# First x tiles and first weight columns loaded ahead of the recurrence constants in a two-stage hybrid block

## The chip, the cores and the metric

One core of a Trainium2 chip runs the whole kernel. The metric is the device time of one execution in microseconds. Engines are named as in the profile: PE (TensorE, with PEld for its weight loads), DVE (VectorE), ACT (ScalarE), POOL (GpSimd), and SP (SyncE, which issues nearly all DMAs).

## The reference

The input is x, 2048 tokens of width 1024, in float32; 16 learned meta tokens are put ahead of it and dropped at the end. One layer is computed:

```
h += rms_norm(W_out [RG-LRU | forgetting attention | RWKV-7](W_in rms_norm(h)))
h += rms_norm(W_down(gelu(g) * v)),   [g | v] = causal_dwconv3(W_up rms_norm(h))
```

W_in has 3080 columns: 512 feed the RG-LRU group ("a"), 3 x 512 are queries, keys and values ("q", "k", "v") with 8 forget-gate columns, and 1024 feed the RWKV-7 group ("c"). The RG-LRU and RWKV-7 groups are recurrences over the tokens.

## The kernel before, in words

Matrix products in float32 precision are made of three matmuls (`mm3`): each operand is split into a high part (rounded to fp32r by ACT) and a low part (the rest, by DVE).

The input projection works in three parts of the tokens, each with two blocks of up to 400 tokens (part 0: the meta rows and tiles x1 to x3, then tiles x4 to x6). `w_in_norm` calls `norm_transpose` for every tile of 128 tokens: a load into a slot of the pool "nt" (four slots, shared with raw weight columns), the sum of squares on ACT (L118), the reciprocal root by three Newton steps on DVE (`rstd_from`, L85 to L94; with `core.apart` the steps run on POOL, L90 and L91), the scaling by the root and the gain `g_pre` on DVE (L130), eight 128x128 transposes on PE (L143), and the evacuation into a high part (ACT, L149) and a low part (DVE, L150).

`w_in_part` is a generator that then runs over the columns: first the forget gate (`w_in_gate`, L287 and L288), then units of 128 columns. For a unit, `w_in_weights` loads the columns (L165), splits them (L166 on ACT, L167 on DVE) and, in part 0, keeps both halves in DRAM for the later parts (L216). `w_in_step` multiplies them with each block (24 matmuls, L172 to L174) and stores the result in a scratch in DRAM (L243 for "a" and "c"). The last two units run block by block together.

The driver builds the first `READY = 13` steps of that generator, then the constants of the recurrences (`attn_consts`, `rwkv_consts`, `lru_consts`, `columns`: short vectors loaded by SP, L848, transposed on PE, L854, copied on DVE, L855; weights at L895 to L898 and L1355; the series of `lru_consts` on DVE, L1368 and L1369), and then goes on with the generator while the recurrences (L993 to L1440; their first matmul is L1034) are woven in beside it. They take their intermediate tiles from the pool "rp", where the tag "rw_sc" has two slots. Attention, output projection and the feed-forward stage follow.

The order in which each engine issues is not the order of this code alone: a scheduler with a timeline of its own arranges the instructions, under their dependencies and in the order written where it sees no reason against it. Each engine then works its list in order. `tc.issue_after(ins)` puts what is written inside it behind `ins` on that instruction's engine.

The lines that order the start are these:

```
following = w_in_norm(core, pools, ps_mm, x, meta, g_pre, 0)
...
units = w_in_part(core, pools, ps_mm, a["w_in"], blocks, scr, part)
for _ in range(READY if part == 0 else 0):
    next(units)
if part == 0:
    attn_consts(core)
    rk = rwkv_consts(...)
```

Of the kernel before, what the change touches and what calls it, by code (L numbers as in the profile page):

```python
# [8 lines left out]
F32 = mybir.dt.float32  # L9
# [3 lines left out]
AF = mybir.ActivationFunctionType  # L13
# [108 lines left out]
def norm_transpose(core, pools, psum, src, rows, gain, pieces):  # L122

    nc = core.nc
    xt = pools["nt"].tile([P, D], F32, tag="nt_x", name=core.n("xt"))
    nc.sync.dma_start(xt[:rows], src)
    junk = pools["st"].tile([P, D], BF16, tag="stv", name=core.n("xj"), bufs=1)
    v = pools["nt"].tile([P, 6], F32, tag="rs", name=core.n("rs"))
    rs = rstd_of(core, v[:rows], xt[:rows], D, junk[:rows])
    nc.vector.scalar_tensor_tensor(xt[:rows], xt[:rows], rs, gain[:rows], op0=ALU.mult, op1=ALU.mult)  # L130
    transpose_split(core, psum, xt, rows, pieces)
# [21 lines left out]
def split_load(core, pool, raws, src, shape, tag):  # L153

    hi = pool.tile(shape, F32R, tag=tag + "h", name=core.n(tag + "h"))
    lo = pool.tile(shape, F32R, tag=tag + "l", name=core.n(tag + "l"))
    load_parts(core, raws, src, hi[:], lo[:])
    return hi, lo


def load_parts(core, raws, src, hi, lo):

    pool, tag, bufs = raws
    raw = pool.tile(list(hi.shape), F32, tag=tag, name=core.n("raw"), bufs=bufs)
    core.loaded = core.nc.sync.dma_start(raw[:], src)  # L165
    core.nc.scalar.activation(hi, raw[:], AF.Copy)  # L166
    core.nc.vector.tensor_tensor(lo, raw[:], hi, op=ALU.subtract)  # L167


def mm3(nc, out, ah, al, bh, bl, first, last, more=False):  # L170
# [3 lines left out]
    nc.tensor.matmul(out, al, bh, start=False, stop=last, skip_group_check=more)  # L174
# [12 lines left out]
def w_in_norm(core, pools, psum, x, meta, gain, part):  # L187
    blocks = []
    for b, tl in enumerate(w_in_tokens(part)):
# [4 lines left out]
        blocks.append((t0, n, tl, hi, lo))  # L194
    for t0, n, tl, hi, lo in blocks:
        for s, rows in tl:
            src = meta if s < META else x[s - META : s - META + rows, :]
            norm_transpose(core, pools, psum, src, rows, gain, [(hi, lo, s - t0, 0, rows)])
    return blocks

# [6 lines left out]
def w_in_weights(core, pools, w_in, c0, scr, part):  # L207

    if part == 0:
        src = w_in[:, c0 : c0 + P].rearrange("(k p) c -> p k c", p=P)  # L210
        pair = split_load(core, pools["w"], (pools["nt"], "nt_x", None), src, [P, KD, P], "w")
# [8 lines left out]
def w_in_step(core, pools, psum, weights, block, kind, c0, scr):  # L220
# [6 lines left out]
    for k in range(KD):  # L227
        mm3(nc, ps[:, :n], wh[:, k], wl[:, k], hi[:, k], lo[:, k], k == 0, k == KD - 1)
# [68 lines left out]
def w_in_part(core, pools, psum, w_in, blocks, scr, part):  # L297
    yield from w_in_gate(core, pools, psum, w_in, blocks, scr, part)
# [11 lines left out]
    for kind, c0 in units[:-2]:  # L310
# [4 lines left out]

    last = [(w_in_weights(core, pools, w_in, c0, scr, part), kind, c0) for kind, c0 in units[-2:]]
    for block in blocks:
        for w, kind, c0 in last:
            step(w, block, kind, c0)
        yield  # L320
# [1592 lines left out]

WIDE = (0, 5)
# [61 lines left out]
def hybrid_block_kernel(ctx: ExitStack, tc: tile.TileContext, args, out):  # L1976
# [25 lines left out]
    with ExitStack() as p1:  # L2002
# [7 lines left out]
        with ExitStack() as p1a:  # L2010
            ps_mm = pool(p1a, "ps_mm", 5, space=PSUM)
            g_pre = spread(pool(p1a, "gpre", 1), a["norm_mix_pre"], "g_pre")
# [3 lines left out]
            following = w_in_norm(core, pools, ps_mm, x, meta, g_pre, 0)  # L2016
            for part in range(3):
# [6 lines left out]
                units = w_in_part(core, pools, ps_mm, a["w_in"], blocks, scr, part)  # L2024
                for _ in range(READY if part == 0 else 0):
                    next(units)
                if part == 0:
                    attn_consts(core)
                    rk = rwkv_consts(
# [14 lines left out]
                    columns(core, gp, ps_ae, [a["ffn_conv"].rearrange("i (r p) -> (i r) p", p=P)], "", cw)  # L2044
                    R = Rwkv(core, rp, dp, ps_rw, ps_ae, scr, rk)
# [168 lines left out]
```

## Time and profile before

| what | value |
|---|---|
| runs | 3072.16 us median of 3 (3068.99 to 4877.26) |
| profiled execution, span from first to last instruction | 3071.8 us |
| PE busy | 2921.6 us, 95% |
| PE weight loads busy | 2495.2 us, 81% |
| DVE busy | 2054.8 us, 67% |
| ACT busy | 1482.3 us, 48% |
| POOL busy | 1358.8 us, 44% |
| DMA, mean over the span | 173 GB/s |

How to read it: the span is the profiled execution's own time, and no other time of that execution is given. A busy share is a mean over stages with different limits; a stage's own limit is read from a window of it. In a row of a group or of the timeline, "out<-in" are the tiles written and read, and the bracket names what ended the idle time before the instruction. SPq is SP's queue of DMA issues. Lines such as L130 are lines of the kernel before.

### The profile page before, as it was taken

What the parts mean: (1) busy time and instruction counts of PE and PEld (TensorE: products, weight loads), DVE (VectorE), ACT (ScalarE), POOL (GpSimd) and SP (SyncE); (2) the same over time, 40 slices, a digit from 0 to 9 for tenths busy, and PEclk for the clock granted to TensorE, in tenths of its full rate; (3) what the DMA queues carried; (4) which work ended last, traced back from release to release, by engine and by line L of the source; (5) the groups of instructions that cost most, each with busy time, mean ns of one, the idle gap of its engine ahead of it and who ended that gap; (6) DMA issues with size and microseconds to landing.
All of it is one profiled execution on the core that took longest, in us unless ns stands there. A gap on an engine that the chain in (4) does not pass through costs nothing. (4 is left out here: it accounts for less than half of the span.)

```text
span 3071.8 us, 52793 instructions
## 1 busy us (share of the span) xinstructions
PE 2921.6 (95%) x18694; PEld 2495.2 (81%) x18694; DVE 2054.8 (67%) x3934; ACT 1482.3 (48%) x2853; POOL 1358.8 (44%) x1589
## 2 busy tenths in 40 slices
PE   6999999999989999999989899999999999999998
PEld 6998898888876654665558899999999998787876
DVE  5268645656667785556635788888778786547766
ACT  4245332443336553555534656666566665324333
POOL 1001121122114555667842457445655444547765
PEclk9998999999988898999999999999999999999999
DMA  6776578466654346535245555566777765435444
GB/s 211 244 237 207 161 244 287 156 211 204 196 153 94 88 104 199 133 99 122 62 129 173 168 182 180 169 201 208 214 215 216 219 189 171 161 104 171 149 160 144
DMA packets 467818, 532.58 MB, mean 173 GB/s; under 512 B 85488, under 2 KB 355514, under 8 KB 466000
## 3 DMA queue, kind: packets, MB, share of 16 engines
q1 hardware_dynamic: 467168, 528.81, 56.5%
q8 instruction: 147, 2.41, 0.3%
q14 instruction: 119, 0.97, 0.1%
q0 software_dynamic: 384, 0.39, 0.0%
HBM read 369.11 MB, written 159.95 MB: 172 GB/s over the span
## 5 line engine op out<-in xcount | busy, mean ns | idle before, releaser
L172 PE MATMUL psu<-xo,uw 128*128 128x344 f32 x1848 | 589.9, 323 | 16.7 <-ACT xo L1594 6.9
L173 PE MATMUL psu<-xo,uw 128*128 128x344 f32 x1848 | 592.6, 321 | 0.0
L174 PE MATMUL psu<-xo,uw 128*128 128x344 f32 x1848 | 582.9, 320 | 0.0
L172 PE MATMUL psp<-xh,wh 128*128 128x384 f32 (+2 forms) x1152 | 383.6, 333 | 4.1 <-ACT wh L166 2.4
L174 PE MATMUL psp<-xh,wl 128*128 128x384 f32 (+2 forms) x1152 | 380.7, 331 | 3.5 <-DMA wl<-scr_wk 3.5
L173 PE MATMUL psp<-xl,wh 128*128 128x384 f32 (+2 forms) x1152 | 380.5, 330 | 0.0
L172 PEld LDWEIGHTS psu<-xo,uw 128*128 128x128 f32 x1848 | 346.9, 188 | 20.3 <-ACT xo L1594 7.1
L1595 DVE TENSOR_TENSOR uw<-uq,uw 128x512 fp32r<-128x512 f32 x341 | 316.2, 933 | 70.3 <-ACT uw L1594 63.7
L173 PEld LDWEIGHTS psu<-xo,uw 128*128 128x128 f32 x1848 | 347.9, 188 | 0.3 <-DVE xo L1595 0.3
L174 PEld LDWEIGHTS psu<-xo,uw 128*128 128x128 f32 x1848 | 346.5, 188 | 0.0
L1594 ACT ACTIVATE uw<-uq 128x512 fp32r<-128x512 f32 x462 | 287.9, 627 | 110.1 <-PE psu L174 48.7
L686 ACT ACTIVATE p<-sc,bias 128x512 f32<-128x512 f32 (+4 forms) x352 | 195.8, 590 | 178.5 <-PE sc L682 146.3
L1725 DVE SCALAR_TENSOR_TENSOR uy<-psu,ffn_cols,uy 128x342 f32<-128x342 f32 (+1 forms) x396 | 223.9, 567 | 60.7 <-ACT uy L1723 59.1
L559 DVE TENSOR_REDUCE mc<-mx 128x1 f32<-128x512 f32 (+6 forms) x352 | 190.3, 565 | 100.9 <-PE mx L554 75.8
L1731 POOL TENSOR_TENSOR uy<-uy,uy 128x342 f32<-128x342 f32 (+1 forms) x132 | 140.6, 1065 | 253.2 <-DVE uy L1725 77.4
L725 POOL TENSOR_TENSOR acc<-acc,p 128x512 f32<-128x512 f32 (+3 forms) x208 | 221.8, 1068 | 60.3 <-ACT p L686 23.9
L1595 POOL TENSOR_TENSOR uw<-uq,uw 128x512 fp32r<-128x512 f32 x121 | 177.9, 1470 | 125.0 <-ACT uw L1594 92.7
L174 PEld LDWEIGHTS psp<-xh,wl 128*128 128x128 f32 x1152 | 222.1, 193 | 13.0 <-issue 6.1
L172 PEld LDWEIGHTS psp<-xh,wh 128*128 128x128 f32 x1152 | 222.1, 193 | 10.7 <-issue 4.0
L173 PEld LDWEIGHTS psp<-xl,wh 128*128 128x128 f32 x1152 | 222.1, 193 | 7.6 <-issue 5.5
L1595 DVE TENSOR_TENSOR fo<-u,fo 128x896 fp32r<-128x896 f32 x88 | 112.6, 1279 | 121.3 <-ACT fo L1594 121.3
L1594 ACT ACTIVATE fo<-u 128x896 fp32r<-128x896 f32 x88 | 81.1, 922 | 206.3 <-POOL u L1841 106.8
(465 smaller groups left out, 6470.4 us busy)
## 6 DMA issues: line engine op xcount, KB each, us to landing
uq<-scr_us SPq DMA_DIRECT2D x220, 256.0 KB
uq<-in_ffn_up_dram SPq DMA_DIRECT2D x209, 256.0 KB
wl<-scr_wk SPq DMA_DIRECT2D x48, 512.0 KB
wh<-scr_wk SPq DMA_DIRECT2D x48, 512.0 KB
u<-scr_ff SPq DMA_DIRECT2D x88, 256.0 KB
scr_ff<-uy SPq DMA_DIRECT2D x110, 171.0 KB
raw<-in_w_in_dram SPq DMA_DIRECT2D x24, 512.0 KB
scr_wk<-wh SPq DMA_DIRECT2D x24, 512.0 KB
```

The lines of the kernel that those rows point to most:

```text
L172: nc.tensor.matmul(out, ah, bh, start=first, stop=False, skip_group_check=more)
L173: nc.tensor.matmul(out, ah, bl, start=False, stop=False, skip_group_check=more)
L174: nc.tensor.matmul(out, al, bh, start=False, stop=last, skip_group_check=more)
L559: self.reduced = nc.vector.tensor_reduce(mc[:rows, i, ci : ci + 1], ps[:rows, : e - a], axis=AX.X, op=ALU.max)
L686: last = nc.scalar.activation(p[:rows, :w], ps[:rows, :w], AF.Exp, bias=bias[:rows, j : j + 1])
L725: eng.tensor_tensor(a, ps_[0][0][:rows, c0:n] if start and i == 1 else a, p[:rows, : n - c0], op=ALU.add)
L1594: core.nc.scalar.activation(hi, src, AF.Copy)
L1595: (eng or core.nc.vector).tensor_tensor(lo, src, hi, op=ALU.subtract)
L1725: stt(y[:, :n], src[:, i : n + i], cw[:, 44 * i + cc : 44 * i + cc + 1], y[:, :n], op0=ALU.mult, op1=ALU.add)
L1731: core.pooled = nc.gpsimd.tensor_tensor(v[:, :n], g[:, :n], v[:, :n], op=ALU.mult)
```

## The change

A new function `first_loads` issues the first loads in an order of its own: x1, x2, the gain, x3, the meta rows, the first weight columns, x4 to x6, the second weight columns. The six x tiles go into two tiles of the recurrences' tag "rw_sc" (three x tiles each) in place of slots of "nt". `w_in_norm` takes them from there, treats the meta rows as the last tile of the first block, and sets `core.apart`, so that the Newton steps of part 0 run on POOL. `w_in_part` runs the first two units ("c") ahead of the forget gate in part 0, block by block together. The constants of the recurrences are put behind the last weight transfer, the last matmul and the last weight split that were built when the generator had made its fifth step.

```diff
@@ -119,11 +119,12 @@
     return rstd_from(core.nc, v, ss, width, core.apart)
 
 
-def norm_transpose(core, pools, psum, src, rows, gain, pieces):
+def norm_transpose(core, pools, psum, src, rows, gain, pieces, xt=None):
 
     nc = core.nc
-    xt = pools["nt"].tile([P, D], F32, tag="nt_x", name=core.n("xt"))
-    nc.sync.dma_start(xt[:rows], src)
+    if xt is None:
+        xt = pools["nt"].tile([P, D], F32, tag="nt_x", name=core.n("xt"))
+        nc.sync.dma_start(xt[:rows], src)
     junk = pools["st"].tile([P, D], BF16, tag="stv", name=core.n("xj"), bufs=1)
     v = pools["nt"].tile([P, 6], F32, tag="rs", name=core.n("rs"))
     rs = rstd_of(core, v[:rows], xt[:rows], D, junk[:rows])
@@ -150,20 +151,21 @@
             nc.vector.tensor_tensor(lo[:, ks, ds_], ps[:, :, ss_], hi[:, ks, ds_], op=ALU.subtract)
 
 
-def split_load(core, pool, raws, src, shape, tag):
+def split_load(core, pool, raws, src, shape, tag, raw=None):
 
     hi = pool.tile(shape, F32R, tag=tag + "h", name=core.n(tag + "h"))
     lo = pool.tile(shape, F32R, tag=tag + "l", name=core.n(tag + "l"))
-    load_parts(core, raws, src, hi[:], lo[:])
+    load_parts(core, raws, src, hi[:], lo[:], raw)
     return hi, lo
 
 
-def load_parts(core, raws, src, hi, lo):
+def load_parts(core, raws, src, hi, lo, raw=None):
 
     pool, tag, bufs = raws
-    raw = pool.tile(list(hi.shape), F32, tag=tag, name=core.n("raw"), bufs=bufs)
-    core.loaded = core.nc.sync.dma_start(raw[:], src)
-    core.nc.scalar.activation(hi, raw[:], AF.Copy)
+    if raw is None:
+        raw = pool.tile(list(hi.shape), F32, tag=tag, name=core.n("raw"), bufs=bufs)
+        core.loaded = core.nc.sync.dma_start(raw[:], src)
+    core.parted = core.nc.scalar.activation(hi, raw[:], AF.Copy)
     core.nc.vector.tensor_tensor(lo, raw[:], hi, op=ALU.subtract)
 
 
@@ -171,7 +173,7 @@
 
     nc.tensor.matmul(out, ah, bh, start=first, stop=False, skip_group_check=more)
     nc.tensor.matmul(out, ah, bl, start=False, stop=False, skip_group_check=more)
-    nc.tensor.matmul(out, al, bh, start=False, stop=last, skip_group_check=more)
+    return nc.tensor.matmul(out, al, bh, start=False, stop=last, skip_group_check=more)
 
 
 
@@ -184,7 +186,7 @@
     return [tiles[a:e] for a, e in zip(cuts, cuts[1:])]
 
 
-def w_in_norm(core, pools, psum, x, meta, gain, part):
+def w_in_norm(core, pools, psum, x, meta, gain, part, landed={}):
     blocks = []
     for b, tl in enumerate(w_in_tokens(part)):
         t0 = tl[0][0]
@@ -192,23 +194,60 @@
         hi = pools["xn"].tile([P, KD, n], F32R, tag=f"xh{b}", name=core.n("xh"))
         lo = pools["xn"].tile([P, KD, n], F32R, tag=f"xl{b}", name=core.n("xl"))
         blocks.append((t0, n, tl, hi, lo))
+    core.apart = bool(landed)
     for t0, n, tl, hi, lo in blocks:
-        for s, rows in tl:
+        for s, rows in tl[1:] + tl[:1] if t0 == 0 else tl:
             src = meta if s < META else x[s - META : s - META + rows, :]
-            norm_transpose(core, pools, psum, src, rows, gain, [(hi, lo, s - t0, 0, rows)])
+            norm_transpose(core, pools, psum, src, rows, gain, [(hi, lo, s - t0, 0, rows)], landed.get(s))
+    core.apart = False
     return blocks
 
 
+def first_loads(core, pools, gpool, rpool, x, meta, gain, w_in):
+
+    nc = core.nc
+    landed = {}
+    tiles = [t for tl in w_in_tokens(0) for t in tl]
+    g = gpool.tile([P, D], F32, name="g_pre")
+
+    def rows_of(some):
+        if len(some) > 1:
+            three = rpool.tile([P, 3, D], F32, tag="rw_sc", name=core.n("x0"), bufs=2)
+        else:
+            three = pools["nt"].tile([P, 1, D], F32, tag="nt_x", name=core.n("xt"))
+        for i, (s, rows) in enumerate(some):
+            nc.sync.dma_start(three[:rows, i], meta if s < META else x[s - META : s - META + rows, :])
+            landed[s] = three[:, i]
+            yield
+
+    early, late, ahead = rows_of(tiles[1:4]), rows_of(tiles[4:7]), []
+    for _ in range(2):
+        next(early)
+    nc.sync.dma_start(g[:], gain.rearrange("(o n) -> o n", o=1).broadcast_to([P, D]))
+    for rest in (early, rows_of(tiles[:1])):
+        for _ in rest:
+            pass
+    for i in range(2):
+        raw = pools["nt"].tile([P, KD, P], F32, tag="nt_x", name=core.n("raw"))
+        c0 = 2056 + P * i
+        nc.sync.dma_start(raw[:], w_in[:, c0 : c0 + P].rearrange("(k p) c -> p k c", p=P))
+        ahead.append(raw)
+        if i == 0:
+            for _ in late:
+                pass
+    return g, landed, ahead
+
+
 def w_in_kept(scr, c0):
 
     return scr["wk"][c0 // P]
 
 
-def w_in_weights(core, pools, w_in, c0, scr, part):
+def w_in_weights(core, pools, w_in, c0, scr, part, raw=None):
 
     if part == 0:
         src = w_in[:, c0 : c0 + P].rearrange("(k p) c -> p k c", p=P)
-        pair = split_load(core, pools["w"], (pools["nt"], "nt_x", None), src, [P, KD, P], "w")
+        pair = split_load(core, pools["w"], (pools["nt"], "nt_x", None), src, [P, KD, P], "w", raw)
     else:
         pair = [pools["w"].tile([P, KD, P], F32R, tag=s, name=core.n(s)) for s in ("wh", "wl")]
     for t, kept in zip(pair, w_in_kept(scr, c0)):
@@ -225,7 +264,7 @@
     t0, n, tl, hi, lo = block
     ps = psum.tile([P, 512], F32, tag="mm", name=core.n("psp"))
     for k in range(KD):
-        mm3(nc, ps[:, :n], wh[:, k], wl[:, k], hi[:, k], lo[:, k], k == 0, k == KD - 1)
+        core.multiplied = mm3(nc, ps[:, :n], wh[:, k], wl[:, k], hi[:, k], lo[:, k], k == 0, k == KD - 1)
     if kind in ("q", "k"):
         sc = 0.125 if kind == "q" else 1.0
         r0 = c0 - (512 if kind == "q" else 1024)
@@ -294,8 +333,7 @@
     yield
 
 
-def w_in_part(core, pools, psum, w_in, blocks, scr, part):
-    yield from w_in_gate(core, pools, psum, w_in, blocks, scr, part)
+def w_in_part(core, pools, psum, w_in, blocks, scr, part, ahead=()):
     units = [("c", 2056 + P * i) for i in range(8)] + [("a", P * i) for i in range(4)]
     units += [(s, c + P * i) for s, c in (("k", 1024), ("v", 1536), ("q", 512)) for i in range(4)]
     waiting = [None]
@@ -307,17 +345,22 @@
             waiting[0]()
         waiting[0] = after
 
-    for kind, c0 in units[:-2]:
+    def both(some, raws=(None, None)):
+        pairs = [(w_in_weights(core, pools, w_in, c0, scr, part, raw), kind, c0) for (kind, c0), raw in zip(some, raws)]
+        for block in blocks:
+            for w, kind, c0 in pairs:
+                step(w, block, kind, c0)
+            yield
+
+    if part == 0:
+        yield from both(units[:2], ahead)
+    yield from w_in_gate(core, pools, psum, w_in, blocks, scr, part)
+    for kind, c0 in units[2 if part == 0 else 0 : -2]:
         w = w_in_weights(core, pools, w_in, c0, scr, part)
         for block in blocks:
             step(w, block, kind, c0)
         yield
-
-    last = [(w_in_weights(core, pools, w_in, c0, scr, part), kind, c0) for kind, c0 in units[-2:]]
-    for block in blocks:
-        for w, kind, c0 in last:
-            step(w, block, kind, c0)
-        yield
+    yield from both(units[-2:])
 
 
 def scratch(tc, ctx, core):
@@ -1911,6 +1954,8 @@
 READY = 13
 PACE = 2.0
 
+BEGUN = 4
+
 WIDE = (0, 5)
 
 LATE = 8
@@ -2009,11 +2054,12 @@
         rp = pool(rec, "rp", 1, **right)
         with ExitStack() as p1a:
             ps_mm = pool(p1a, "ps_mm", 5, space=PSUM)
-            g_pre = spread(pool(p1a, "gpre", 1), a["norm_mix_pre"], "g_pre")
+            g_pool = pool(p1a, "gpre", 1)
             pools = {"xn": pool(p1a, "xn", 1), "nt": pool(p1a, "nt", 4), "w": pool(p1a, "w", 2), "st": pool(p1a, "st", 2)}
             sums = up_sums(core, pool(p1a, "us", 1), a["ffn_up"], scr, EARLY)
             split_out = w_out_split(core, pools["nt"], a["w_out"], scr)
-            following = w_in_norm(core, pools, ps_mm, x, meta, g_pre, 0)
+            g_pre, landed, ahead = first_loads(core, pools, g_pool, rp, x, meta, a["norm_mix_pre"], a["w_in"])
+            following = w_in_norm(core, pools, ps_mm, x, meta, g_pre, 0, landed)
             for part in range(3):
                 blocks = following
                 if part == 0:
@@ -2021,11 +2067,16 @@
                     nc.vector.memset(zeros[:], 0.0)
                     for r in range(0, A_ROWS + C_ROWS, P):
                         nc.gpsimd.dma_start(scr["p"][r : r + P, 0:PAD], zeros[:])
-                units = w_in_part(core, pools, ps_mm, a["w_in"], blocks, scr, part)
+                units = w_in_part(core, pools, ps_mm, a["w_in"], blocks, scr, part, ahead)
                 for _ in range(READY if part == 0 else 0):
                     next(units)
+                    if _ == BEGUN:
+                        begun = [t.ins for t in (core.loaded, core.multiplied, core.parted)]
                 if part == 0:
                     attn_consts(core)
+                    behind = ExitStack()
+                    for ins in begun:
+                        behind.enter_context(tc.issue_after(ins))
                     rk = rwkv_consts(
                         core, gp, ps_ae,
                         {
@@ -2042,6 +2093,7 @@
                         },
                     )
                     columns(core, gp, ps_ae, [a["ffn_conv"].rearrange("i (r p) -> (i r) p", p=P)], "", cw)
+                    behind.close()
                     R = Rwkv(core, rp, dp, ps_rw, ps_ae, scr, rk)
                     beside = Beside(PACE)
                 for i, _ in enumerate(units, READY + 1 if part == 0 else 1):
```

## The prediction

> **What bounds the kernel now.** The first part of the page gives TensorE (PE) 95% of the span. So a change pays only where PE is idle, and what it delays costs only if PE then stands. The busy table by stages shows where the idle time of the start lies.
>
> ```profile
> span 3071.8 us, 52793 instructions
> PE 2921.6 (95%) x18694; PEld 2495.2 (81%) x18694; DVE 2054.8 (67%) x3934; ACT 1482.3 (48%) x2853; POOL 1358.8 (44%) x1589
> ...
> 0.00:10.00 10.00, 0.00 (x0) 0.00 (x0) 5.92 (x47) 4.00 (x6) 6.29 (x17) 1.00 0.75 242
> ...
> 20.00:38.00 18.00, 8.48 (x36) 6.98 (x36) 17.01 (x69) 8.98 (x18) 0.00 (x0) 1.00 0.69 208
> 38.00:140.00 102.00, 102.00 (x567) 101.98 (x566) 28.04 (x40) 30.19 (x43) 0.41 (x1) 1.00 0.71 232
> ```
>
> Columns: stretch, its length, busy time of PE, weight load, VectorE (DVE), ScalarE (ACT), GpSimd (POOL), clock, DMA share, GB/s. From 38 us on PE has no gap for 100 us. From 20 to 38 us VectorE is busy 17.0 of 18.0 us: the preparation of the x tiles and the recurrence constants share it. The timeline says what opens the dense stretch.
>
> ```profile
> 36.29 1.94 PE L143 MATMUL pst<-ident,xt 128*128 128x128 f32 x8 [4.00 <-DVE lruv L1369]
> ...
> 37.89 0.68 PE L287 MATMUL psf<-xh,fw 128*128 128x400 f32 x1
> ```
>
> The columns are start, length, engine, line, operands and count. The seventh x tile is transposed, and at 37.89 the first matmul of the input projection (the gate) begins. That moment is what the change aims at. It can gain at most 37.9 us, 1.2% of the span. A measurement of this kernel tells about 2% from no change, 61 us, so "faster" in that sense is out of reach of the start alone.
>
> **The change part by part.** The order in which the changed kernel issues on each engine is known from its listing; here is what it holds, priced with rows of before.
>
> *The loads.* SyncE issues x1, x2, the gain, x3, the meta rows, weights 1, x4, x5, x6, weights 2. The constants, earlier mixed in, come after these.
>
> ```profile
> xt<-in_x_dram SPq DMA_DIRECT2D x16, 512.0 KB
> ...
> raw<-in_w_in_dram SPq DMA_DIRECT2D x24, 512.0 KB
> ...
> q0 software_dynamic: 384, 0.39, 0.0%
> ...
> 8.00:10.00 2.00, 0.00 (x0) 0.00 (x0) 0.61 (x7) 1.57 (x3) 0.48 (x1) 1.00 1.04 343
> 10.00:12.00 2.00, 0.25 (x3) 0.28 (x4) 2.00 (x11) 1.37 (x3) 1.87 (x7) 1.00 0.35 87
> ...
> 34.00:36.00 2.00, 0.00 (x0) 0.00 (x0) 2.00 (x8) 0.00 (x0) 0.00 (x0) 1.00 1.00 309
> ```
>
> Nine loads of 512 KB (4.72 MB), 0.07 MB of meta rows and GpSimd's 0.39 MB of padding make 5.17 MB until weights 2 have landed. The first 10 us moved 242 GB/s, 2.42 MB. The other 2.75 MB take 8.0 us at the 343 GB/s of 8 to 10 us, 8.9 us at the 309 of 34 to 36 us, where weight columns were loading too, and 13.2 us at the 208 of 20 to 38 us. So weights 2 land at 18.0, 18.9 or 23.2 us; I take 18.9, since this queue is never empty.
>
> *What waits for weights 2.* Both ScalarE and VectorE split weights 1 and then weights 2 before they go on: the first x tile's normalisation (L130) stands on VectorE behind the low part of weights 2, and ScalarE evacuates no transpose before their high part. The early x tiles are thus held by the last load.
>
> ```profile
> 29.27 1.06 ACT L166 ACTIVATE wh<-raw 128x1024 fp32r<-128x1024 f32 x1 [2.68 <-DMA raw<-in_w_in_dram]
> 30.36 1.23 DVE L167 TENSOR_TENSOR wl<-raw,wh 128x1024 fp32r<-128x1024 f32 x1
> ...
> 26.27 1.28 DVE L130 SCALAR_TENSOR_TENSOR xt<-xt,rs,g_pre 128x1024 f32<-128x1024 f32 x1
> ...
> L150 DVE TENSOR_TENSOR xl<-pst,xh x14: 214/681/692, 14.0 to 38.9; 128x512 fp32r<-128x512 f32 x12, 128x64 fp32r<-128x64 f32 x2
> ```
>
> VectorE is through with weights 2 at 18.9 + 1.06 + 1.23 = 21.2 us (20.3 to 25.5).
>
> *Newton on GpSimd.* Each tile's three Newton steps move from VectorE to six GpSimd operations.
>
> ```profile
> 15.56 0.29 POOL L365 TENSOR_SCALAR_AFFINE_SELECT futureb<-futureb 128x128 bf16<-128x128 bf16 x1
> ...
> L90 POOL TENSOR_SCALAR rs<-rs x24: 333/343/366, 1222.1 to 1567.4; 128x1 f32<-128x1 f32 x21, 2x1 f32<-2x1 f32 x3
> ...
> L91 POOL TENSOR_SCALAR rs<-rs x24: 256/267/1190, 1223.7 to 1568.7; 128x1 f32<-128x1 f32 x21, 2x1 f32<-2x1 f32 x3
> ```
>
> GpSimd's own preparation ends at 15.85 us and stays in its queue; 24 operations for four tiles add 12 x 0.343 + 12 x 0.267 = 7.3 us, so they end at 23.2. The four tiles run interleaved, and x1 is finished three operations before the end, at 22.4. That is later than 21.2: the first normalisation starts at 22.4.
>
> On GpSimd the trace has single L91 operations of 1.19 us against a median of 0.267. The Trainium skill, "GPSIMD Engine Reference", section "Specifications", says that GpSimd shares its SBUF interface with VectorE and collides with VectorE instructions that have two SBUF inputs. By it L167 and L130, which have two, would each hold up one such operation: two longer by 0.9 us would put the sum at about 3077 instead of 3075. The trace agrees with slow single operations, not with their cause.
>
> *From there to the first projection matmul.* VectorE's listing holds four normalisations (4 x 1.28 = 5.1, to 27.5 us), then the eight low parts of the first block (6 x 0.68 + 2 x 0.21 = 4.5) with nine small operations of x4 to x6 between them (1 us), to 33.0. The third of those tiles' seeds stands behind three low parts, at about 30.3, and GpSimd then needs 6 x 0.343 + 5 x 0.267 = 3.4 us until x4 is finished, at 33.7. Three normalisations end at 37.5. PE's listing has all transposes ahead of the first projection matmul, so the last tile's 1.94 us come on top: 39.5 us, against 37.89. That is a loss of 1.6 us. The bounds: with weights 2 at 18.0 and no wait for GpSimd, 20.3 + 5.1 + 4.5 + 1.0 + 3.8 + 1.9 = 36.6, and 35.6 if the small operations hide: a gain of 2.3; with weights 2 at 23.2, 41.8: a loss of 3.9.
>
> *The constants behind unit five.* They leave the idle start and come while PE is dense. (A unit is one set of 128 weight columns, 48 matmuls over two blocks.)
>
> ```profile
> 14.14 0.27 PE L854 MATMUL pscol<-ident,rows 22*128 22x22 f32 x1 [1.40 <-DMA rows<-in_rwkv_ln_b_dram]
> ...
> 16.10 0.63 PE L914 MATMUL psspr<-ident,gat 128*4 128x128 f32 x2
> ...
> 20.55 0.25 PE L854 MATMUL pscol<-ident,rows 16*128 16x16 f32 x1 [1.25 <-DMA rows<-in_lru_lambda_dram]
> ...
> 25.76 0.45 PE L854 MATMUL pscol<-ident,rows 128*128 128x128 f32 x1 [0.48 <-DMA rows<-in_ffn_conv_dram]
> ...
> 29.50 0.26 PE L854 MATMUL pscol<-ident,rows 4*128 4x4 f32 x1
> ```
>
> These transposes sum to 1.86 us; they overlap their neighbours, so I take 1.0 (0 to 1.9). Their VectorE work lies beside PE: VectorE has 28.0 busy of 102 us in that stretch. Their 26 DMAs pass through SyncE's queue, which waits in every unit:
>
> ```profile
> 73.31 0.46 SPq L165 DMA_DIRECT2D raw<-in_w_in_dram  x1
> 75.72 4.54 SPq L243 DMA_DIRECT2D scr_p<-stp  x2
> ...
> 81.90 0.45 SPq L165 DMA_DIRECT2D raw<-in_w_in_dram  x1
> ```
>
> A unit takes 81.90 - 73.31 = 8.6 us, and half of it SyncE stands at L243. At no more than the 0.46 us that a weight load's issue takes, 12 us over ten units, the DMAs are hidden; without that cover a weight load would come up to 12 us late.
>
> *The recurrences.* Their first matmul (L1034) moves from behind 14.85 units in PE's order to behind 16.85, since the constants' transposes stand only behind units 12 to 14.5. Two units are 17 us. Both listings have put 911 recurrence matmuls by unit 48, and behind the last projection 657 stand before and 625 after. The lag is recovered in the order, so I price it at 0. The bounds are +17 us (not recovered in time) and a gain in the tail.
>
> ```profile
> L174 PE MATMUL psp<-xh,wl x1152: 274/337/736, 42.5 to 896.0; 128*128 128x384 f32 x96, 128*128 128x256 f32 x64, 128*128 128x400 f32 x32
> ...
> L1321 PE MATMUL rps<-rwsg,g_up x36: 275/379/564, 373.2 to 1147.5; 128*128 128x256 f32 x32, 128*128 128x64 f32 x4
> ```
>
> The tail runs from 896 to 1147.5, 251 us; 32 of 657 matmuls fewer are at most 12 us of it.
>
> *The sum* against the profiled execution: 3071.8 + 1.6 + 1.0 = 3074.4. The median of the runs, 3072.16, stands 0.4 above this span; so 3075 us.
>
> **The rivals.**
>
> *A, a real gain.* The loads come fast, GpSimd keeps up, and fewer recurrence steps are left behind the projections: -2.3 at the start, 0 for the constants, -12 in the tail: 3058. For it: the tail of before has idle PE time, and VectorE no longer runs the constants in the first 38 us. Against it: attention fills PE in the tail anyway (93% busy in 1000 to 1100).
>
> ```profile
> 900.00:1000.00 100.00, 85.72 (x815) 61.08 (x815) 80.48 (x226) 52.35 (x115) 41.99 (x69) 0.86 0.53 119
> 1000.00:1100.00 100.00, 92.61 (x814) 59.71 (x809) 78.86 (x212) 58.59 (x126) 56.61 (x91) 0.90 0.34 85
> ```
>
> *B, GpSimd late.* GpSimd's queue begins with the padding DMAs, and it waits for them to land:
>
> ```profile
> 9.52 1.74 POOL L2023 DMA_DIRECT2D scr_p<-zeros  x3 [1.70 <-DMA scr_p<-zeros]
> ```
>
> The last of them was issued by 11.26, when the DMA engines ran empty (share 0.35 from 10 to 12 us). If now they wait until the loads are through at 18.9, everything on GpSimd slips by 7.6 us, the start with it: 3082. Against it: the earlier ones got through by 9.5 us, while the share was 1.04. The Trainium skill, "DMA: Bandwidth & Descriptors", section "Queues, rings and completion order", says that each DMA engine takes turns between its queues; by it the padding gets its turn and this rival falls away.
>
> *C, slower through the recurrences.* The lag of 17 us is not made up: recurrence chains run through VectorE, which has only 20% idle in 900 to 1000 us (80.48 of 100, above), so a lag there is hard to make up. Then what follows moves by the lag: 3075 + 17 = 3092. It decides when the counts of recurrence steps behind the same projection unit stay apart. Over 2% (3134) it would need a lag of seven units.
>
> *D, it does not do what it says.* The x tiles land early but nothing uses them before weights 2: that is inside the forecast. With the constants fully hidden too, the time is 3072 to 3074.
>
> **How the numbers follow.** Forecast (with D) 0.48: its own range is 3071.8 - 2.3 to 3071.8 + 3.9 + 1.9, rounded outward for the run's own spread, 3068 to 3080. A 0.26 at 3058, B 0.10 at 3082, C 0.16 at 3092, a quarter of it beyond 2%. The range reaches to A and C: 3054 to 3098. Faster by over 2% 0.01, within 0.95, slower 0.04.
>
> **What would show it.** Right: ScalarE idle before the second L166 form until weights 2 land at 18 to 23 us; the first L130 at 21 to 26 us; the first projection matmul between 36 and 42 us; constants' transposes (L854's code) between 110 and 140 us; the recurrence's first L1034 some 17 us later than before. Wrong: a first projection matmul before 33 us, for then the order did not hold the x tiles back; or a difference of more than 10 us that arises behind 200 us, for then the steps of the start are beside the point and the re-ordered recurrences decide.

## The result and the profile after

The changed kernel takes 3084.73 us (median; 3074.32 to 3092.05), the kernel before, on the same chip, 3071.76. The ratio is 1.0035 with an interval of [1.0023, 1.0047]; a second group of runs gave 1.0018 [1.0003, 1.0033]. So the change costs some 6 to 11 us. The forecast was 3075 in a range of 3054 to 3098, class "within 2%". Class and range hold, but the sum is short by about 8 us (by the ratio; 10 by the medians), and 3084.73 lies outside the 3068 to 3080 that the forecast gave itself: only the reach of its range to rival C takes it in.

The first part of the page of after, and its busy table for the stretches shown of before:

```profile
span 3085.0 us, 52799 instructions
PE 2913.3 (94%) x18694; PEld 2499.6 (81%) x18694; DVE 2044.1 (66%) x3892; ACT 1481.2 (48%) x2853; POOL 1371.6 (44%) x1631
...
0.00:10.00 10.00, 0.00 (x0) 0.00 (x0) 4.43 (x40) 3.67 (x6) 6.65 (x18) 1.00 0.79 262
...
20.00:38.00 18.00, 9.60 (x48) 8.97 (x49) 14.35 (x27) 8.26 (x17) 11.89 (x26) 0.84 0.58 190
38.00:140.00 102.00, 102.00 (x572) 102.00 (x572) 26.66 (x38) 26.76 (x38) 0.00 (x0) 0.99 0.65 213
900.00:1000.00 100.00, 82.08 (x750) 59.77 (x745) 71.66 (x197) 44.88 (x99) 35.01 (x55) 0.74 0.47 104
1000.00:1100.00 100.00, 89.46 (x875) 60.44 (x875) 79.11 (x216) 56.58 (x122) 51.97 (x84) 0.93 0.35 87
```

PE was not given more work: it is idle for 3085.0 - 2913.3 = 171.7 us, against 3071.8 - 2921.6 = 150.2 before. The start, up to 38 us, adds only 4.4 of these 21.5. From 38 to 140 us PE again has no gap. From 900 to 1000 us PE is busy for 82.08 us against 85.72, at a granted clock of 0.74 against 0.86; the work there is not quite the same, since after is some 12 us behind by then.

The timeline of after shows the start (start, length, engine, line; in brackets the idle time before and what ended it):

```profile
9.61 1.06 POOL L2069 DMA_DIRECT2D scr_p<-zeros  x2 [0.42 <-DMA scr_p<-zeros]
18.42 1.06 ACT L168 ACTIVATE wh<-raw 128x1024 fp32r<-128x1024 f32 x1 [5.24 <-DMA raw<-in_w_in_dram]
19.51 1.23 DVE L169 TENSOR_TENSOR wl<-raw,wh 128x1024 fp32r<-128x1024 f32 x1 [5.07 <-ACT wh L168]
22.09 3.69 DVE L131 SCALAR_TENSOR_TENSOR x<-x,rs,g_pre 128x1024 f32<-128x1024 f32 x3 [1.35 <-POOL rs L91]
33.13 2.48 DVE L131 SCALAR_TENSOR_TENSOR x<-x,rs,g_pre 128x1024 f32<-128x1024 f32 x2 [1.77 <-POOL rs L91]
33.31 2.44 POOL L90 TENSOR_SCALAR rs<-rs 128x1 f32<-128x1 f32 x1
34.57 5.00 PE L144 MATMUL pst<-ident,x 128*128 128x128 f32 x24 [4.91 <-DVE x L131]
36.14 1.29 DVE L131 SCALAR_TENSOR_TENSOR x<-x,rs,g_pre 128x1024 f32<-128x1024 f32 x1 [0.53 <-POOL rs L91]
39.32 0.43 PE L174 MATMUL psp<-xh,wh 128*128 128x400 f32 x1
```

Read downward, this is the chain that the prediction walked. ScalarE and VectorE stand idle for 5.24 and 5.07 us until weights 2 have landed, although the first x tiles are there; then GpSimd's Newton steps hold VectorE for 1.35 and 1.77 us; the first projection matmul comes at 39.32 us.

How far after is behind before, at the same place of the work (PE's projection matmuls counted, 48 to a step; worked out from both traces, the second column from the second profile of after):

| place | after | after, 2nd profile |
|---|---|---|
| end of step 12 | +0.3 | +1.1 |
| step 24 | -4.6 | -3.9 |
| step 36 | +2.1 | +3.2 |
| step 72, the last | +12.1 | +6.8 |
| first matmul of the feed-forward stage | +11.5 | +6.6 |

Step 24 is ahead mainly because PE has no idle time from step 12 to step 24 (before: 2.4 us) and six recurrence matmuls fewer have come (96 against 102; counted are all matmuls that write `rps` or `eps`). The loss arises between steps 24 and 72, in the stretch where recurrences run between projections, and is then carried to the end. Busy tables for the same work, from the end of step 24 to the end of step 72 and from there to the first matmul of the feed-forward stage, before and then after:

```profile
277.71:896.25 618.54, 594.22 (x5532) 536.30 (x5531) 370.60 (x930) 247.93 (x485) 123.07 (x200) 0.96 0.62 203
896.25:1678.52 782.27, 728.28 (x4235) 467.44 (x4234) 497.49 (x1110) 391.94 (x781) 440.13 (x595) 0.94 0.47 124
```

```profile
273.11:908.32 635.21, 602.31 (x5602) 543.54 (x5602) 380.95 (x969) 251.63 (x490) 119.31 (x202) 0.95 0.62 199
908.32:1689.97 781.65, 716.85 (x4169) 466.67 (x4170) 496.72 (x1093) 391.58 (x781) 438.03 (x593) 0.94 0.48 124
```

By step 72 after has done 70 matmuls more: 64 of the recurrences' (3207 against 3143 in all) and the 6 that were missing at step 24. PE is busy there for 8.1 us more, and idle for 8.6 us more. Behind step 72 the work done early does not come back: PE is busy for 11.4 us less, and the stretch is as long (781.65 against 782.27 us), because its idle time rises from 54.0 to 64.8 us. The second profile of after agrees (600.22 busy in 629.18, then 718.18 in 782.07). Most of that growth are PE's waits for attention's loads, 4.9 us in all before and 13.5 after; the longest of before, and then the two longest of after (engine, line and releaser: us in total, times, longest):

```profile
PE mx L554 <- DMA k<-scr_kh: 3.3, 2, 1.8
```

```profile
PE mx L597 <- DMA k<-scr_cl: 6.5, 4, 2.5
PE sc L724 <- DMA q<-scr_qh: 5.3, 1, 5.3
```

PE's longest waits from 262 to 480 us, before and then after:

```profile
PE rps L1138 <- DVE rwbk L1132: 2.7, 1, 2.7
PE pst L143 <- DVE xl L150: 1.7, 1, 1.7
```

```profile
PE rps L1219 <- DVE rwxu L1235: 4.9, 2, 4.0
PE eps L1107 <- DVE rwix L78: 4.8, 1, 4.8
PE pst L144 <- DVE stl L274: 3.0, 1, 3.0
PE rps L1152 <- ACT rww L1367: 2.3, 1, 2.3
```

The first recurrence matmul comes 19 us later, and one of these waits, the 4.8 us of L1107 that end at 286.48, falls where VectorE works off low parts (L151) of the next part's tokens between the steps that L1107 needs. The 3.0 us of L144 belong to those tokens themselves, and the longest wait of L1219 ends at 442 us, behind steps of the recurrences on VectorE. These waits come with the lag, and they are not the loss by themselves: late_rec below, with the same lag, has 15.6 us of listed waits in this window, against 17.9 here and 7.8 before, and is faster than before. The busy table, before and then after:

```profile
270.00:480.00 210.00, 202.29 (x1795) 183.90 (x1794) 124.62 (x304) 81.76 (x146) 39.53 (x64) 0.96 0.64 208
900.00:1100.00 200.00, 178.33 (x1621) 120.79 (x1620) 159.34 (x436) 110.94 (x240) 98.60 (x159) 0.88 0.43 102
```

```profile
270.00:480.00 210.00, 191.98 (x1661) 173.59 (x1663) 122.29 (x289) 83.46 (x148) 37.45 (x64) 0.94 0.64 207
900.00:1100.00 200.00, 171.54 (x1624) 120.20 (x1620) 150.78 (x411) 101.45 (x221) 86.97 (x139) 0.84 0.41 96
```

In both stretches PE is busy for 7 to 10 us less and has a clock 0.02 to 0.04 lower (the second profile of after: 192.78 at 0.93 and 171.87 at 0.83). The windows are fixed in time while the work has shifted, so these are not to be added up to the loss; they say where it is.

### The profile page after: what moved, and what is told of

It is laid out like the page before. It is cut to its first block, busy times and chain, and to the rows that moved or that the text cites. A ratio compares the mean times of both kernels' runs of the same rounds, so it can differ in the third digit from the quotient of the medians.

```text
span 3085.0 us, 52799 instructions
## 1 busy us (share of the span) xinstructions
PE 2913.3 (94%) x18694; PEld 2499.6 (81%) x18694; DVE 2044.1 (66%) x3892; ACT 1481.2 (48%) x2853; POOL 1371.6 (44%) x1631
## 5 line engine op out<-in xcount | busy, mean ns | idle before, releaser
L602 DVE TENSOR_REDUCE mc<-mx 128x1 f32<-128x512 f32 (+5 forms) x352 | 190.0, 566 | 109.1 <-PE mx L597 79.9
```

The lines of the kernel that those rows point to most:

```text
L602: self.reduced = nc.vector.tensor_reduce(mc[:rows, i, ci : ci + 1], ps[:rows, : e - a], axis=AX.X, op=ALU.max)
```

## The experiments

Three causes were in question at the outset: the recurrences' lag, the constants' work in the dense stage, and the start's loads and Newton steps (the first four expectations call the lag that the held constants bring theory 1, and the start theory 3; theory 2 is that every re-ordering costs about as much). "Lag" is the step of PE's order in which the first recurrence matmul stands (before 14.85, after 16.85). The first projection matmul is the gate's where the gate comes first. Each ratio is against runs of the kernel before on the same chip; since the chips of the three groups differ by up to 0.3% for that kernel (medians 3074.9, 3075.9, 3068.2), only ratios are compared between groups.

| kernel | constants | lag to step | first projection matmul, us | ratio |
|---|---|---|---|---|
| after | held | 16.85 | 39.3 | 1.0035 [1.0023, 1.0047] |
| after_again | held | 16.85 | 39.9 | 1.0018 [1.0003, 1.0033] |
| consts_free | free | 14.85 | 48.7 | 1.0015 [1.0002, 1.0028] |
| consts_only | held | 16.85 | 33.9 | 1.0009 [0.9991, 1.0028] |
| newton_dve | held | 16.85 | 31.5 | 1.0007 [0.9994, 1.0021] |
| free_swap_dve | free | 14.85 | 31.7 | 0.9998 [0.9980, 1.0015] |
| late_start | free | 14.85 | 48.3 | 1.0011 [0.9996, 1.0026] |
| late_rec1 | free | 15.85 | as before | 0.9990 [0.9978, 1.0002] |
| late_rec | free | 16.85 | 37.9 | 0.9971 [0.9954, 0.9988] |
| late_rec3 | free | 17.79 | as before | 1.0009 [0.9993, 1.0025] |
| late_rec8 | free | 23.04 | as before | 1.0101 [1.0070, 1.0133] |
| held_late | held | 16.85 | as consts_only | 0.9955 [0.9939, 0.9970] |
| early_late | free | 16.85 | 32.6 | 0.9951 [0.9933, 0.9968] |

### Parts of the change undone

**consts_free**: after, with the constants not held back.

```
-                        behind.enter_context(tc.issue_after(ins))
+                        behind.enter_context(nullcontext())
```

> The changed kernel, but the recurrence constants are not held behind unit five. In its listing the first recurrence matmul stands behind 14.85 projection units again, as before the change, and the recurrence counts equal those of before up to unit 36. The copy of the RWKV columns now stands on VectorE ahead of the first normalisation, so the first projection matmul should come 2 to 4 us later than the changed kernel's 39.3, at 41 to 43 us. Theory 1 (the held constants delay the recurrences by two units, and that costs the 12 us that arise behind unit 12): about 3074 to 3077 us, and PE idle between units 12 and 72 as in before. Theory 2 (every re-ordering costs about that much, wherever it comes from): about 3085. Theory 3 (GpSimd Newton and the new loads do it): 3085 to 3089.

The first projection matmul came at 48.7 us, later than any theory had it. The timeline says why:

```profile
37.41 0.17 DVE L898 COPY lru_cols<-pscol 128x16 f32<-128x16 f32 x1 [5.49 <-PE pscol L897]
```

A copy of constants, whose transpose on PE waits 6.94 us for its rows to land, stands in VectorE's queue ahead of the last x tiles, and VectorE is idle before it for 5.49 us. In this order of loads, with Newton's steps on GpSimd, holding the constants is thus needed. Yet 9.7 us lost by step 12 became only 4.6 us at the end (0.0015 of 3075): the first sign that the start is not passed on whole.

**consts_only**: before, with the constants held behind the fifth step, and none of the new loads (shown in part).

```
                     next(units)
+                    if _ == 4:
+                        begun = [t.ins for t in (core.loaded, core.multiplied, core.parted)]
...
                 attn_consts(core)
+                    behind = ExitStack()
+                    for ins in begun:
+                        behind.enter_context(tc.issue_after(ins))
```

> The kernel before with only the constants held behind the fifth step; loads and Newton steps as before. First recurrence matmul behind 16.85 units, as in the changed kernel. VectorE loses the constants' work from the first 38 us, so the first projection matmul should come at 33 to 37 us instead of 37.9. Theory 1: the late recurrences cost 12 us all the same, 3072 - 3 + 12 = about 3080. Theory 2: anything from 3065 to 3085. Theory 3: 3068 to 3070, the earlier start alone.

No difference that can be told (1.0009, interval across 1). Its step 12 ends 4.5 us earlier than before's, and that is gone at the end.

**newton_dve**: after, with the Newton steps back on VectorE.

```
-    core.apart = bool(landed)
+    core.apart = False
```

> The changed kernel with the Newton steps of part 0 on VectorE. The listing then puts the first normalisations and the first block's evacuations ahead of weights 2; weights 2 (landing at 18.4) still stand ahead of the meta rows' normalisation. First projection matmul at 30 to 32 us instead of 39.3. The recurrences stay as late as in the changed kernel. Theory 1: 3085 - 8 = about 3077. Theory 2: 3065 to 3085, without relation to the start. Theory 3: at or under 3068.

The first projection matmul came at 31.5 us, as expected: Newton's steps on GpSimd cost 7.8 us at the start. At the end the ratio is 1.0007 against after's 1.0035 and 1.0018, so by these values 3 to 9 us of it arrive; its interval is clear of the first group's and overlaps the second's.

**free_swap_dve**: constants free, Newton on VectorE, and the last x tiles loaded behind weights 2 instead of between the two (the last of the three edits is shown).

```
-        if i == 0:
-            for _ in late:
-                pass
+    for _ in late:
+        pass
```

> The changed kernel with three edits: constants not held back, Newton steps on VectorE, and weights 2 loaded ahead of x4 to x6. First projection matmul at 29 to 32 us; first recurrence matmul behind 14.85 units. Theory 1: 3072 - 6 to - 8 = 3064 to 3066, faster than both. Theory 2: anything from 3062 to 3085. Theory 3: 3064 to 3066 too.

31.7 us at the start, 12.1 us ahead of before at step 72, and nothing at the end: 0.9998. The busy table from 1130 to 1160 us, before and then this kernel, shows one place where the lead is lost:

```profile
1130.00:1160.00 30.00, 23.59 (x104) 12.19 (x102) 21.42 (x54) 13.21 (x28) 10.77 (x21) 0.83 0.39 78
```

```profile
1130.00:1160.00 30.00, 18.12 (x76) 9.82 (x75) 13.66 (x35) 8.33 (x18) 10.37 (x15) 0.77 0.72 175
```

PE is busy for 18.12 of 30 us at a clock of 0.77, VectorE for 13.66, while the DMA share is 0.72 against 0.39. It is a wait for a load of attention's:

```profile
PE mx L646 <- DMA mt<-scr_cl: 8.2, 1, 8.2
```

At the same place (L604 there) before waits 0.5 us.

The expectations of these four were made for a kernel before of some 3072 us; on this chip it took 3074.9, so 3 us are to be added. Theory 3 then misses consts_free (3088 to 3092, measured 3079.4) and newton_dve (at or under 3071, measured 3079.5). Theory 1 fits these two, but has consts_only at 3083 (measured 3074.8), the upper end of its interval. Both have free_swap_dve at 3067 to 3069 (measured 3072.3), at or below its interval's lower end. Theory 2 gave one narrow figure, about 3088 for consts_free, and missed it. So none of the three holds throughout.

### The start and the lag by themselves

**late_start**: before, with eight passes over the last x tile of part 0 added on VectorE (`again` is 8 for that tile and 0 for all others).

```
+    for _ in range(again):
+        nc.vector.scalar_tensor_tensor(xt[:rows], xt[:rows], 1.0, xt[:rows], op0=ALU.mult, op1=ALU.max)
```

> The kernel before, with its last x tile held up on VectorE: eight more passes of scalar_tensor_tensor over 128 x 1024 that leave it unchanged (about 1.15 us each by the normalisations' rows, so 9 us), nothing else. The first projection matmul should move from 37.9 to 46-48 us, with the order of the later work nearly as before. Theory 'the start is passed on': everything behind shifts with it, total +8 to +10 us, ratio 1.0026 to 1.0033. Rival 'the later stages soak it up' (slope of about a third, as the first four runs suggest): +2 to +4 us, ratio 1.0007 to 1.0013, with the delay still there at projection step 12 and mostly gone by the end of attention.

The first matmul moved to 48.3 us, step 12 was 10.5 us late, step 72 ended with before's (896.3 both), and the median is 2.4 us longer: 1.0011 [0.9996, 1.0026]. The value is that of "soaked up"; "passed on" (1.0026 to 1.0033) lies at the interval's upper end and beyond. How it is soaked up was not shown.

**late_rec**: before, with the recurrences entered two steps later and nothing else.

```
-                    if i == READY + 1:
+                    if i == READY + (3 if part == 0 else 1):
```

> The kernel before, with the recurrences entered two projection steps later in the program (first recurrence matmul in step 16.85 of the order, as in the kernel after, instead of 14.85); the constants stay at the start. Theory 'the recurrences' lag is what the change costs': step 72 of the projections ends 5 to 12 us later than before and the total is +4 to +10 us, ratio 1.0013 to 1.0033. Rival 'the lag is made up in the order, as the prediction had it': 0 to +2 us, ratio 0.9995 to 1.0007, step 72 within 4 us of before; then the constants' transposes and copies in the dense stage, or the start, carry the loss.

Both theories missed. It is faster: 0.9971 [0.9954, 0.9988], some 9 us. So the theory that after's lag of two steps is by itself the loss falls. From the end of step 24 to the end of step 72 it has as many PE matmuls as after, and gets through them sooner:

```profile
271.36:891.63 620.27, 592.29 (x5601) 534.76 (x5600) 385.91 (x969) 253.30 (x490) 123.66 (x202) 0.96 0.63 204
```

Of the 14.9 us that after takes longer there, PE is busy for 10.0, at a clock of 0.95 against 0.96, and idle for 4.9; of the 8.9 us of after's second profile, which ran on the same chip as late_rec, busy for 7.9. Behind step 72 late_rec has the idle time of after (64.0 us).

**late_rec8**: the same with READY + 9.

> As the last, with the recurrences entered eight steps later (first recurrence matmul in step 23.04 of the order; 782 recurrence matmuls by step 48 against 876 before). Theory 'the lag is what costs': a loss that grows with the lag, four times that of two steps if it is proportional, +16 to +40 us, ratio 1.005 to 1.013. Rival 'made up in the order': under +5 us, ratio below 1.0016.

1.0101: 31 us, inside what a lag that costs was to give. At step 72 this kernel is 27.1 us ahead of before, since recurrence matmuls have not come yet by then (2807 against 3143), and it is 19.8 us behind at the stage after attention: the work left over is done behind the projections. Only a large lag works like rival C of the prediction.

**after_again**: after once more, no edit.

> The kernel after once more, to see which of the differences between the first two profiles come again. If the loss is the program's own: ratio 1.002 to 1.005, step 25 of the projections about 14 us earlier than before, step 72 about 12 us later, attention late by 11 to 13 us all through. If the profile of after was an execution at the long end of its spread: ratio 1.000 to 1.002, and the differences at steps 25 and 72 come out otherwise by 8 us or more.

1.0018 lies among the values of the second expectation, 1.000 to 1.002, just under the first; the places are nearer to the first: step 25 is 12.5 us ahead, step 72 6.8 us late, and the waits of 262 to 480 us are the same three (5.6, 5.3 and 3.4 us). Both groups exclude 1, so the loss is the program's own, with a size of 6 to 11 us by the two ratios.

### Which order

**early_late**: free_swap_dve and late_rec together.

> The kernel after with its constants not held back, Newton steps on VectorE and the second weight columns ahead of the last x tiles (as free_swap_dve), and the recurrences entered two projection steps later (as late_rec). First projection matmul 30-33 us against 37.9. If the two gains add: -2 (free_swap_dve) and -10 us (late_rec) make 3060 to 3067, ratio 0.995 to 0.9975. If the earlier start is swallowed by a lower granted clock: ratio 0.9965 to 0.999 with a mean clock 0.002 to 0.004 under that of before. Rival 'every order draws its own lot, without a rule': anywhere in 0.997 to 1.004.

0.9951 [0.9933, 0.9968], 10 to 21 us, within what adding the gains was to give. The gains of the two kernels, 0.6 and 8.9 us by their ratios, add up to the near end of that. This kernel is faster than before and after.

**late_rec1** and **late_rec3**: late_rec with READY + 2 and READY + 4.

> The kernel before with the recurrences entered one projection step later (first recurrence matmul in step 15.85 of the order). If the gain of late_rec belongs to the lag: between before and late_rec, -2 to -8 us, ratio 0.9975 to 0.9993. Rival 'own lot': outside of that, 0.9995 to 1.004 or below 0.997.

> The kernel before with the recurrences entered three steps later (step 17.79 of the order). A smooth course through -10 us at two steps and +32 us at eight gives -8 to 0 us, ratio 0.9975 to 1.000. Rival 'own lot': 1.001 to 1.005, or below 0.9965.

0.9990 fits a smooth course; 1.0009 does not fit well behind 0.9971 at two steps, though its interval still reaches into the smooth course. With lags of 1, 2, 3 and 8 steps the ratios are 0.9990, 0.9971, 1.0009, 1.0101; those of 1 and 3 steps cannot be told from 1, and no rule for the small lags can be read from the four.

**held_late**: consts_only and late_rec together.

> The kernel before with both: recurrences entered two steps later and the constants held behind the fifth step; its recurrence matmuls stand nearly as in late_rec and consts_only (first in step 16.85; 326 against 323 by step 30). Theory 'it is the held constants that cost, not the lag': like consts_only, 3073 to 3081 us, ratio 0.999 to 1.002, with a mean granted clock of 0.965 to 0.969; late_rec had 0.9971 with the constants at the start. Rival 'the held constants cost nothing by themselves': like late_rec, 3063 to 3069, ratio 0.9955 to 0.9985.

0.9955 [0.9939, 0.9970]: the theory that held constants cost falls as well. This kernel and consts_only have the same first recurrence step, the same lead at step 12 (4.6 and 4.5 us) and the same counts of recurrence matmuls by the ends of steps 24, 30, 48 and 60 (96, 624, 1694, 2352), and they are 0.5% apart. The counts differ elsewhere: 968 here against 992 there by step 36, 3215 against 3205 by step 72. Between the ends of steps 24 and 72 PE here is busy for 591.93 us over 5608 matmuls at a clock of 0.97, there for 604.30 us over 5598 at 0.95. So a difference in the recurrences' order that hardly shows in counts like those the prediction used can go with as much time as the whole effect of the change. (The two ran on different chips; a chip that treats the two kernels differently isn't excluded.) In the stretches where after lost, held_late has:

```profile
270.00:480.00 210.00, 198.12 (x1768) 178.41 (x1770) 122.67 (x299) 85.70 (x153) 37.71 (x67) 0.95 0.66 220
900.00:1100.00 200.00, 182.63 (x1667) 125.98 (x1667) 154.13 (x422) 119.42 (x255) 103.23 (x175) 0.88 0.41 98
```

From 900 to 1100 us its PE is busy for 182.63 us at 0.88, after's for 171.54 at 0.84. Its longest waits in 262 to 480 us are of the kinds of after's three longest (4.3, 3.2 and 1.6 us), so those kinds of wait are not what sets the two apart.

## Why the prediction was right or wrong

*The loads: right.* Weights 2 were forecast for 18.9 us; ScalarE took them at 18.42. VectorE was through with them at 19.51 + 1.23 = 20.7, forecast 21.2.

*Newton on GpSimd: right.* First normalisation forecast 22.4, measured 22.09; x4 ready 33.7, measured 33.13; normalisations ended 37.5, measured 36.14 + 1.29 = 37.4. The slow single operations came as well: 2.44 us for one L90, whose longest was 0.366 before, while VectorE ran L131 beside it. The rule of the Trainium skill ("GPSIMD Engine Reference", "Specifications") says that GpSimd collides with VectorE instructions that have two SBUF inputs, and L131 has two; the trace agrees that the operation beside it was slow, and does not show the cause. At most 0.53 us of that one reached VectorE, so the 3077 that the prediction gave by this rule was no better a sum.

*First projection matmul: right.* Forecast 39.5, measured 39.32 (39.9 in the second profile), a loss of 1.4 us against 1.6. Of that 0.3 to 1.1 us were left at step 12. newton_dve shows that this small sum is made of two large ones: the new loads bring the matmul to 31.5 us, 6.4 ahead of before, and Newton's steps on GpSimd take 7.8 back.

*The constants: right in size, late in time.* They were to stand between 110 and 140 us:

```profile
L897 PE MATMUL pscol<-ident,rows x4: 220/233/271, 148.3 to 170.9; 22*128 22x22 f32 x1, 16*128 16x16 f32 x1, 128*128 128x128 f32 x1, 4*128 4x4 f32 x1
...
L957 PE MATMUL psspr<-ident,gat x2: 272/272/272, 152.7 to 152.8; 128*4 128x128 f32 x2
```

They came at 148 to 171 us and take 4 x 0.23 + 2 x 0.27 = 1.5 us, forecast 1.0 (0 to 1.9). The window was at odds with the prediction's own figures: it had the transposes behind units 12 to 14.5, and at 8.6 us a unit from 39.5 on that is 143 to 164 us. SyncE issued the loads for the second to fourth transpose only at 148 to 164 us, between its weight loads.

*Rival B fell:* the last padding DMA was issued by 9.61 + 1.06 = 10.67 us, long before weights 2 had landed at 18.4 us. By the rule in "DMA: Bandwidth & Descriptors", "Queues, rings and completion order", of the Trainium skill, each DMA engine takes turns between its queues, and the trace agrees. *Rival A fell* at its first term, since the start gained nothing, and at its last: 64 recurrence matmuls fewer were left behind the projections, and the stretch behind them was no shorter.

*The recurrences: the step that failed.* The lag itself came as walked: first recurrence matmul 19 us later. The first row is before's, the others are after's:

```profile
L1034 PE MATMUL eps<-rwwa,wa_up x72: 272/376/502, 174.5 to 978.2; 64*128 64x256 f32 x64, 64*128 64x64 f32 x8
...
L1077 PE MATMUL eps<-rwwa,wa_up x72: 272/376/480, 193.4 to 981.1; 64*128 64x256 f32 x64, 64*128 64x64 f32 x8
...
L1364 PE MATMUL rps<-rwsg,g_up x36: 217/379/635, 393.7 to 1151.2; 128*128 128x256 f32 x32, 128*128 128x64 f32 x4
...
L176 PE MATMUL psp<-xh,wl x1152: 274/337/882, 39.8 to 908.0; 128*128 128x384 f32 x96, 128*128 128x256 f32 x64, 128*128 128x400 f32 x32
```

"The lag is recovered in the order, so I price it at 0" was the wrong term. The counts do agree by step 48 (1694 in both traces, by the wider count used here), and the last projection is still 12 us later (908.0 against 896.0; 6.8 us in the second profile). By then after has done 64 recurrence matmuls more than before, and from step 24 on PE was busy for 8.1 us and idle for 8.6 us more; behind the last projection the early work gains nothing, since PE waits there instead, mostly for attention's loads. The prediction named a difference of more than 10 us that arises behind 200 us as the sign that its start is beside the point. The first profile shows it (+0.3 at step 12, +11.5 at the feed-forward stage), the second does not quite (+1.1 and +6.6). Nor is the start wholly beside the point: newton_dve, with the same lag and nearly the same counts, lacks 3 to 9 us of after's loss. Rival C's mechanism was not it either: two steps of lag alone gain 9 us. A count says how much PE work stands where, and nothing of what PE then waits for, nor at which clock it works. That the time still lies in the stated range is owed to the room left for rivals, not to the sum. Bounds of about ±0.5% for "the order changes" are what these runs support (0.9951 to 1.0035 for lags up to three steps).

*What stays open:* why PE takes longer between steps 24 and 72 in after than in late_rec, with as many matmuls and the same lag. The granted clock goes with it: over all runs its mean is lower in after (0.966 of 16 and of 12 runs) than in before (0.970, 0.970 and 0.972 on the three chips), though single runs overlap. Within the kernels that have 12 runs or more, 0.001 of clock goes with 1.0 to 2.8 us, so 0.004 would go with 4 to 11 us, the size of the loss. But this is an association, and it doesn't hold between kernels: newton_dve has 0.965 at a ratio of 1.0007, and free_swap_dve 0.967 at 0.9998. What sets the clock in these stretches was not tested.

## What to carry to other kernels

Counts of work on the bound engine don't price a re-ordering, and neither did the waits of a single window here; give "the order changed" a term of its own, in this kernel ±0.5%. Work moved ahead of a stage saves nothing there if that stage then waits for something else: PE had 11.4 us less to do behind the projections, and the stretch stayed as long. A gain at the start isn't to be carried to the end one to one: 10.5 us late cost 2.4, 12.1 us ahead at the end of the projections gave nothing. Loads that go first help only if no engine's queue has an instruction ahead of their users that waits for a later load.

## What the hardware showed

In after's start PE waits 4.91 us for the last x tiles, and works at half its clock for some time behind that pause:

```profile
30.00:35.00 5.00, 0.43 (x2) 0.46 (x3) 3.23 (x6) 0.00 (x0) 5.00 (x13) 0.72 0.38 105
35.00:38.00 3.00, 3.00 (x16) 3.00 (x15) 2.47 (x4) 1.79 (x3) 1.01 (x2) 0.50 0.00 0
38.00:41.00 3.00, 3.00 (x18) 3.00 (x18) 3.00 (x6) 1.70 (x3) 0.00 (x0) 0.82 0.00 0
41.00:44.00 3.00, 3.00 (x19) 3.00 (x18) 0.02 (x1) 0.03 (x1) 0.00 (x0) 1.00 0.03 5
```

PE pauses, then works at 0.50, and has its full clock again some 5 us later. The Trainium skill, "TensorE: Matmul & The Clock Gate", "Part 1: The HAM clock gate (the "warmup" mystery)", says that a PE that has been idle runs at half rate until about 4 us of sustained matmuls have passed; the trace agrees. The record of the clock doesn't always show it. In late_start it says 1.00 throughout, yet the matmuls' spacing tells:

```profile
48.77 0.54 PE L293 MATMUL psf<-xl,fw 128*128 128x400 f32 x1
49.10 0.54 PE L292 MATMUL psf<-xh,fw 128*128 128x400 f32 x1
...
51.22 0.34 PE L293 MATMUL psf<-xl,fw 128*128 128x400 f32 x1
51.40 0.34 PE L292 MATMUL psf<-xh,fw 128*128 128x400 f32 x1
```

0.33 us apart, then 0.18: about half rate until some 4 us after its transposes began at 46.70. So a wait of PE of this length is to be priced with the slow microseconds behind it, and a granted clock of 1.00 in the record doesn't prove that there were none.
